# MLP up units: three of four results taken from one running PSUM sum

## The chip, the cores and the metric

The kernel runs on one core of a Trainium2 chip. The metric is the device time of one execution in microseconds (us). TensorE (PE) multiplies matrices into PSUM banks, VectorE (DVE) and ScalarE (ACT) read PSUM and SBUF, GpSimd (POOL) works on SBUF alone, and SyncE (SP) issues the DMAs. Each engine takes its own instructions in a fixed order and waits on semaphores for the others.

## The reference

One layer of a hybrid encoder on x of 2048 tokens by 1024 channels: a mixing half (attention, short convolution, pooling) and then the MLP, which is what the change touches:

```python
h2 = rms_norm(x, norm2_g[l])
f = jnp.square(jax.nn.relu(jnp.einsum('bsd,df->bsf', h2, w_mlp1[l])))
x = x + jnp.einsum('bsf,fd->bsd', f, w_mlp2[l])
```

h2 is 2048 x 1024, w_mlp1 1024 x 4096, w_mlp2 4096 x 1024.

## The kernel before

The first half of the span is the mixing half, which the change leaves alone. The MLP works on tokens in two blocks of 1024 (tb 0 and 1), on the 4096 hidden channels in four chunks (c 0 to 3), and in each chunk first on four **up units** (i 0 to 3, `up`, L995), then on four **down units** (`down`, L1021). So there are 64 units, in the order of the list `units` (L974).

Each unit is a 2 x 2 block product by the seven-product scheme of Strassen and Winograd. Its left operands are sums of weight blocks (a11, a12, a22, s1 to s4) and its right operands sums of data blocks (b11, b21, b22, t1 to t4). Every operand is split into two f16 tiles, high and low, and `product` (L907) multiplies high x high, high x low and low x high for four slices of the inner dimension: twelve matmuls of 128x128 by 128x512 into one PSUM bank. A unit is 84 matmuls. The banks are named b[0] to b[3], each with two buffers, so that the next unit can start while one is read out; b[3] has its own pool (pm1), which opens only after the last step of the mixing half (`stats`, L805) has given its PSUM back.

In `up` the four results are c11 = P(a11) + P(a12); u2 and u3, running sums that start from P(a11) + P(s2); and c21. Before the change ScalarE copies P(a11) out of b[0] (L1001), and VectorE adds every further product from its bank to a tile in SBUF (L1003, L1006, L1008, L1012, L1014: five additions). The product P(a12) is added by TensorE to b[0], which still holds P(a11). Banks b[2] and b[3] are each written twice in a unit. Then ScalarE takes relu (L1017) and square (L1018) of each result, and `data_sums` (L891) makes the seven operands of the down units from them: four subtractions on POOL, and for each operand a cast on ScalarE (L861) and a subtraction on VectorE (L862).

The first time a unit's weights are used (tb 0), `load` (L955) fetches four raw blocks, makes the sums on POOL (`weight_sums`, L868) and splits seven operands (ScalarE L864, VectorE L865), and stores them to `wd` in DRAM. In tb 1 it loads the seven tiles from `wd`, in the order of `WORDER` (L49), into a pool of twelve buffers. The data operands of the MLP's input go through `xd` in DRAM the same way, in the order of `OPS` (L357). At four places (`SPILLS`, L48) `prepare_spill` makes the input operands of tb 1 between units of tb 0. Results and temporaries of the up units share one pool of seven SBUF tiles (`tmp`, L855).

The order of instructions on each engine is not the program's: a scheduler sets it, from its own estimate of when each operand will be there. It moves products ahead of others where it thinks that they would wait.

## Time and profile before

| what | us |
|---|---|
| median of 3 runs | 2141.82 |
| lowest and highest of them | 2135.64, 2143.37 |
| the profiled execution | 2138.21 |
| its span (first to last instruction) | 2136.3 |
| PE busy, share of the span | 96% |
| DVE, ACT, POOL busy | 63%, 48%, 27% |

All that follows is read from the one profiled execution, whose own time lies 3.6 us below the median of the runs. A matmul is recorded with its latency, and matmuls overlap, so a matmul's pace is read from how many fit in a stretch and not from its duration. Idle time that a row gives is the engine's idle time just before the row, with the instruction that ended it.

### The profile page before, as it was taken

To read this page: it belongs to the slowest core of one execution; us is meant where nothing else is said; L and a number is where in the kernel's file an instruction comes from. 1 tells how busy PE (TensorE), PEld (TensorE's weight loads), DVE (VectorE), ACT (ScalarE), POOL (GpSimd) and SP (SyncE) were. 2 spreads that over 40 slices of the span, in tenths; PEclk is the share of its full clock that TensorE was granted. 3 is DMA by queue.
4 is the path that set the end of the run, shared out by engine and by line. 5 is a ranking of instruction groups with operands and counts; after the bars stand their busy time and mean duration, and the time that the engine had idled before them with its cause. 6 is when DMAs were issued, how large, how long until landed. Compare 5 with 4: busy or idle time off the path is not lost. (4 is left out here: it accounts for less than half of the span.)

```text
span 2136.3 us, 31619 instructions
## 1 busy us (share of the span) xinstructions
PE 2041.8 (96%) x11072; PEld 1257.2 (59%) x11072; DVE 1337.3 (63%) x2208; ACT 1016.4 (48%) x2028; POOL 575.8 (27%) x441
## 2 busy tenths in 40 slices
PE   8999898999999898998999999999999999999999
PEld 6777787887787687764444444444444444444444
DVE  6676466756676677767768779767743053353354
ACT  5466575666564454535656456456143151150330
POOL 1110012000210133154556456446422031130132
PEclk9999999999999999999999999999999999999999
DMA  9676797668854687493465555548733333333344
GB/s 318 195 226 210 225 276 238 203 219 265 269 177 124 194 263 209 156 340 115 166 228 186 182 198 187 183 148 295 250 121 104 101 102 104 99 99 107 101 151 150
DMA packets 219567, 399.69 MB, mean 187 GB/s; under 512 B 26000, under 2 KB 33296, under 8 KB 219408
## 3 DMA queue, kind: packets, MB, share of 16 engines
q1 hardware_dynamic: 219408, 397.68, 58.0%
q8 instruction: 87, 1.43, 0.3%
q14 instruction: 72, 0.59, 0.1%
HBM read 275.42 MB, written 105.38 MB: 178 GB/s over the span
## 5 line engine op out<-in xcount | busy, mean ns | idle before, releaser
L911 PE MATMUL b_d<-ft_u,s_d 128*128 128x512 f16 x1152 | 264.1, 379 | 7.3 <-ACT ft_u L861 3.2
L911 PEld LDWEIGHTS <-s_d 128*128 128x128 f16 x1536 | 150.2, 98 | 188.6 <-issue 7.3
L911 PEld LDWEIGHTS <-s_u 128*128 128x128 f16 x1536 | 150.7, 98 | 186.1 <-issue 6.8
L911 PE MATMUL b_u<-zt,s_u 128*128 128x512 f16 x1152 | 257.2, 381 | 1.5 <-DVE u2u L1014 0.8
L1032 DVE TENSOR_TENSOR acc<-acc,b_d 128x512 f32<-128x512 f32 x176 | 119.1, 682 | 178.8 <-PE b_d L911 175.6
L911 PEld LDWEIGHTS <-a_u 128*128 128x128 f16 x1152 | 112.8, 98 | 144.6 <-issue 11.4
L911 PEld LDWEIGHTS <-a_d 128*128 128x128 f16 x1152 | 112.6, 98 | 144.8 <-issue 9.8
L911 PE MATMUL b_d<-fb_u,a_d 128*128 128x512 f16 x768 | 183.7, 379 | 4.2 <-DVE acc L1032 2.0
L911 PE MATMUL b_u<-zb,a_u 128*128 128x512 f16 x768 | 176.7, 379 | 1.3 <-ACT u2u L1001 1.3
L611 ACT ACTIVATE sb<-sb,nm 128x640 f32<-128x640 f32 (+4 forms) x128 | 97.5, 762 | 143.2 <-DVE nm L605 135.2
L895 POOL TENSOR_TENSOR t1u<-u2u,c11u 128x512 f32<-128x512 f32 x32 | 43.7, 1366 | 443.4 <-ACT u2u L1018 443.4
L181 PE MATMUL a<-wq,xg 128*128 128x512 f32 x384 | 153.2, 399 | 0.5 <-DVE wq L161 0.4
L180 PE MATMUL a<-wq,xg 128*128 128x512 f32 x384 | 145.0, 402 | 8.5 <-ACT wq L160 8.5
L182 PE MATMUL a<-wq,xg 128*128 128x512 f32 x384 | 152.8, 399 | 0.0
L243 POOL TENSOR_TENSOR acc<-acc,sq 128x512 f32<-128x512 f32 x28 | 37.6, 1342 | 366.2 <-ACT sq L242 351.6
L605 DVE CUSTOM_DVE_ANT_0 sb<-s,b 128x640 f32<-128x640 f32 (+4 forms) x128 | 94.1, 735 | 66.5 <-PE s L602 65.8
L624 DVE SCALAR_TENSOR_TENSOR pp<-pt,pp 128x384 f16<-128x384 f32 (+1 forms) x224 | 104.0, 484 | 44.5 <-ACT pp L623 44.0
L180 PE MATMUL o<-mix,wo 128*128 128x512 f32 x256 | 107.3, 420 | 0.5 <-DVE gb L760 0.5
L180 PE MATMUL cp<-xg,wc 128*128 128x512 f32 x256 | 107.5, 420 | 0.0
L161 DVE TENSOR_TENSOR wq<-rwq,wq 128x512 fp32r<-128x512 f32 x96 | 68.0, 715 | 62.7 <-ACT wq L160 62.7
L623 ACT ACTIVATE pp<-pt 128x384 f16<-128x384 f32 (+1 forms) x224 | 90.8, 430 | 33.3 <-PE pt L622 32.7
L182 PE MATMUL o<-mix,wo 128*128 128x512 f32 x256 | 102.4, 400 | 0.0
(273 smaller groups left out, 4289.8 us busy)
## 6 DMA issues: line engine op xcount, KB each, us to landing
rwq<-w_qkv SPq DMA_DIRECT2D x96, 256.0 KB, 2.9
p<-w1t SPq DMA_DIRECT2D x64, 256.0 KB, 4.1
rwc<-w_cp SPq DMA_DIRECT2D x64, 256.0 KB, 4.3
rwo<-w_out SPq DMA_DIRECT2D x64, 256.0 KB, 4.2
t<-w SPq DMA_DIRECT2D x64, 256.0 KB, 3.8
r_u<-w SPq DMA_DIRECT2D x64, 256.0 KB, 3.0
wd<-s_u SPq DMA_DIRECT2D x64, 256.0 KB, 2.3
r_d<-w SPq DMA_DIRECT2D x64, 256.0 KB, 2.9
```

The source lines that it names most:

```text
L161: behind(ve.tensor_tensor(out=w[:, 1], in0=raw, in1=w[:, 0].bitcast(F32), op=ALU.subtract))
L180: te.matmul(out, ah, bh, start=start, stop=False)
L181: te.matmul(out, ah, bl, start=False, stop=False)
L182: anchor.append(te.matmul(out, al, bh, start=False, stop=stop).ins.name)
L243: gp.tensor_tensor(out=acc, in0=acc, in1=q, op=ALU.add)
L605: ve.tensor_tensor_reduce(out=sb[:, :nk].rearrange("p (e k) -> p e k", e=ne), in0=s[:, :ne, :hk], in1=bi[:, 640 - nk :].rearrange("p (e k) ...
L611: sc.activation(sb[:, :nk], sb[:, :nk], AF.Exp, bias=nmx, scale=-1.0, accum_out=st["l"][:, i, j : j + 1])
L623: sc.activation(pp[:, 0, c0:c1], pt[:, :n], AF.Copy, scale=PSC)
L624: ve.scalar_tensor_tensor(out=pp[:, 1, c0:c1], in0=pt[:, :n], scalar=PSC, in1=pp[:, 0, c0:c1], op0=ALU.mult, op1=ALU.subtract)
L895: gp.tensor_tensor(out=t1, in0=b12, in1=b11, op=ALU.subtract)
L911: te.matmul(bank, w[:, a, q * P : (q + 1) * P], xs[q][:, c], start=start and q == 0 and i == 0, stop=q == n - 1 and i == 2, skip_group_che ...
L1032: ve.tensor_tensor(out=a, in0=a, in1=bk, op=ALU.add)
```

## The change

In the up unit the products come in another order: a11, s1, s2, a12, s3, s4, a22. P(a11), P(s2), P(s3) and P(a22) are now all added up by TensorE in b[0], one after the other. Between them ScalarE copies the state of the sum out: after P(a11) into c11, after P(s2) into u2, after P(s3) into u3; the last state is c21, which the relu reads from b[0]. The bank b[2] holds P(s1) alone, which VectorE adds to u2 and to u3; b[1] holds P(a12), b[3] holds P(s4). Each of the banks b[1] to b[3] is written once in a unit. VectorE has four additions in place of five, ScalarE three copies in place of one. A product into b[0] has to wait until the copy before it has read the bank. The order in which weights and input operands are stored and loaded follows the new order of products for the up units; the down units keep theirs.

```diff
-WORDER = ("a11", "s2", "s3", "s1", "a12", "a22", "s4")
+WORDER = {"u": ("a11", "s1", "s2", "a12", "s3", "s4", "a22"), "d": ("a11", "s2", "s3", "s1", "a12", "a22", "s4")}
...
-    OPS = ("b11", "t2", "t3", "t1", "b21", "t4", "b22")
+    OPS = ("b11", "t1", "t2", "b21", "t3", "b22", "t4")
...
         product(b[0], w["a11"], xs("b11"), True)
+        c11 = tmp("c11" + nm)
+        sc.copy(c11, b[0])
+        product(b[2], w["s1"], xs("t1"), True)
+        product(b[0], w["s2"], xs("t2"), False)
         u2 = tmp("u2" + nm)
         sc.copy(u2, b[0])
-        product(b[1], w["s2"], xs("t2"), True)
-        ve.tensor_tensor(out=u2, in0=b[1], in1=u2, op=ALU.add)
-        product(b[2], w["s3"], xs("t3"), True)
+        product(b[1], w["a12"], xs("b21"), True)
+        ve.tensor_tensor(out=c11, in0=b[1], in1=c11, op=ALU.add)
+        product(b[0], w["s3"], xs("t3"), False)
         u3 = tmp("u3" + nm)
-        ve.tensor_tensor(out=u3, in0=b[2], in1=u2, op=ALU.add)
-        product(b[3], w["s1"], xs("t1"), True)
-        ve.tensor_tensor(out=u3, in0=b[3], in1=u3, op=ALU.add)
-        product(b[0], w["a12"], xs("b21"), False)
-        product(b[2], w["a22"], xs("t4"), False)
+        sc.copy(u3, b[0])
+        ve.tensor_tensor(out=u2, in0=b[2], in1=u2, op=ALU.add)
+        product(b[3], w["s4"], xs("b22"), True)
+        ve.tensor_tensor(out=u3, in0=b[2], in1=u3, op=ALU.add)
+        ve.tensor_tensor(out=u2, in0=b[3], in1=u2, op=ALU.add)
+        product(b[0], w["a22"], xs("t4"), False)
         c21 = tmp("c21" + nm)
-        ve.tensor_tensor(out=c21, in0=b[2], in1=u2, op=ALU.add)
-        product(b[3], w["s4"], xs("b22"), False)
-        ve.tensor_tensor(out=u2, in0=b[3], in1=u2, op=ALU.add)
-        c11 = tmp("c11" + nm)
-        for src, dst in ((b[0], c11), (u3, u3), (c21, c21), (u2, u2)):
+        for src, dst in ((c11, c11), (u3, u3), (u2, u2), (b[0], c21)):
```

The scheduler moves instructions in answer, and three places show how. A matmul row names bank and unit (`b0_u_0_1_2` is b[0] of up unit 2 of chunk 1 in tb 0), data operand and weight operand; of each run of matmuls of one product the first is shown.

TensorE before, where the up units of chunk 1 in tb 0 end and the down units (`_d_`) begin:

```order
L911 MATMUL b0_u_0_1_3_13139<-zb11_0_0_10952,a11_u0_1_3_12886 128x512
...
L911 MATMUL b0_u_0_1_2_12966<-zb21_0_0_11108,a12_u0_1_2_12717 128x512
...
L911 MATMUL b2_u_0_1_2_12968<-zt4_0_0_11141,a22_u0_1_2_12724 128x512
...
L911 MATMUL b3_u_0_1_2_12969<-zb22_0_0_11175,s4_u0_1_2_12734 128x512
...
L911 MATMUL b3_u_0_1_3_13142<-zt1_0_0_11072,s1_u0_1_3_12893 128x512
...
L911 MATMUL b0_d_0_1_0_13312<-fb11_u_0_1_0_12677,a11_d0_1_0_13108 128x512
...
L911 MATMUL b0_u_0_1_3_13139<-zb21_0_0_11108,a12_u0_1_3_12890 128x512
...
L911 MATMUL b2_u_0_1_3_13141<-zt4_0_0_11141,a22_u0_1_3_12897 128x512
...
L911 MATMUL b3_u_0_1_3_13142<-zb22_0_0_11175,s4_u0_1_3_12907 128x512
...
L911 MATMUL b1_d_0_1_0_13313<-ft2_u_0_1_2_13092,s2_d0_1_0_13126 128x512
```

TensorE at the same place now:

```order
L911 MATMUL b0_u_0_1_3_13146<-zb11_0_0_10952,a11_u0_1_3_12892 128x512
...
L911 MATMUL b0_u_0_1_2_12972<-zt2_0_0_11028,s2_u0_1_2_12736 128x512
...
L911 MATMUL b0_u_0_1_2_12972<-zt3_0_0_11108,s3_u0_1_2_12732 128x512
...
L911 MATMUL b3_d_0_1_0_13323<-ft1_u_0_1_0_12695,s1_d0_1_0_13122 128x512
...
L911 MATMUL b0_u_0_1_2_12972<-zt4_0_0_11175,a22_u0_1_2_12729 128x512
...
L911 MATMUL b0_d_0_1_0_13320<-fb11_u_0_1_0_12682,a11_d0_1_0_13115 128x512
...
L911 MATMUL b0_u_0_1_3_13146<-zt2_0_0_11028,s2_u0_1_3_12910 128x512
...
L911 MATMUL b0_u_0_1_3_13146<-zt3_0_0_11108,s3_u0_1_3_12906 128x512
...
L911 MATMUL b0_u_0_1_3_13146<-zt4_0_0_11175,a22_u0_1_3_12903 128x512
...
L911 MATMUL b0_d_0_1_0_13320<-fb21_u_0_1_0_12688,a12_d0_1_0_13119 128x512
```

The steps of unit 2's running sum now stand late and close together: nothing stands between its s2 and its s3 product, and two matmuls of a down unit between s3 and a22.

ScalarE at this place before, from the casts of the spill (`yt`) to the first relu of unit 2's c11:

```order
L861 CAST yt2_1_1_12958<-x2_1_5_1_12930 128x512
L1018 ACTIVATE u3u_0_1_2_13009<-u3u_0_1_2_13009 128x512
L861 CAST yt4_1_1_12962<-x2_1_5_0_12927 128x512
L864 ACTIVATE a11_d0_1_0_13108<-r0_d0_1_0_13098,sw_120 128x512
L864 ACTIVATE a12_d0_1_0_13112<-r1_d0_1_0_13100,sw_120 128x512
L864 ACTIVATE s1_d0_1_0_13115<-s1_d0_1_0_13106,sw_120 128x512
L864 ACTIVATE a22_d0_1_0_13119<-r3_d0_1_0_13104,sw_120 128x512
L864 ACTIVATE s3_d0_1_0_13122<-r2_d0_1_0_13102,sw_120 128x512
L1017 ACTIVATE c11u_0_1_2_13063<-b0_u_0_1_2_12966 128x512
```

ScalarE there now:

```order
L1005 COPY u2u_0_1_2_13014<-b0_u_0_1_2_12972 128x512
L861 CAST fb11_u_0_1_2_13079<-c11u_0_1_2_12988 128x512
L861 CAST yt2_1_1_12964<-x2_1_5_1_12936 128x512
L861 CAST yt4_1_1_12968<-x2_1_5_0_12933 128x512
L864 ACTIVATE a11_d0_1_0_13115<-r0_d0_1_0_13105,sw_120 128x512
L864 ACTIVATE a12_d0_1_0_13119<-r1_d0_1_0_13107,sw_120 128x512
L864 ACTIVATE s1_d0_1_0_13122<-s1_d0_1_0_13113,sw_120 128x512
L1010 COPY u3u_0_1_2_13041<-b0_u_0_1_2_12972 128x512
```

Six instructions now stand between the copies of u2 and of u3 of this unit.

TensorE at the end of the mixing half before, with the products around the two matmul groups of `stats` (ms2_3 and rb23):

```order
L911 MATMUL b2_u_0_0_2_11634<-zt3_0_0_11028,s3_u0_0_2_11442 128x512
...
L248 MATMUL ms2_3_11202<-ones_96,acc23_8559 128x1 x4
...
L911 MATMUL b2_u_0_0_2_11634<-zt3_0_3_11034,s3_u0_0_2_11442 128x512
L256 MATMUL rb23_11223<-ident_87,r1r_11211 128x128 x4
...
L911 MATMUL b3_u_0_0_0_11289<-zt1_0_0_11072,s1_u0_0_0_10898 128x512
```

TensorE there now:

```order
L911 MATMUL b2_u_0_0_2_11636<-zt1_0_0_10989,s1_u0_0_2_11436 128x512
...
L248 MATMUL ms2_3_11202<-ones_96,acc23_8559 128x1 x4
...
L911 MATMUL b2_u_0_0_2_11636<-zt1_0_3_10995,s1_u0_0_2_11436 128x512
...
L911 MATMUL b1_u_0_0_2_11635<-zb21_0_0_11072,a12_u0_0_2_11433 128x512
...
L256 MATMUL rb23_11223<-ident_87,r1r_11211 128x128 x4
...
L911 MATMUL b3_u_0_0_0_11289<-zb22_0_0_11141,s4_u0_0_0_10912 128x512
```

Between ms2_3 and rb23 there stood one matmul, and now stand thirteen, the twelve of the a12 product of unit 2 among them.

## Rows read from the trace of the kernel before

**Rows 1.** The profile's page: span, and busy time of each engine with its share.

```profile
span 2136.3 us, 31619 instructions
PE 2041.8 (96%) x11072; PEld 1257.2 (59%) x11072; DVE 1337.3 (63%) x2208; ACT 1016.4 (48%) x2028; POOL 575.8 (27%) x441
```

**Rows 2.** Busy time in stretches, one per chunk: tb 0's four, then two of tb 1.

```profile
core 0: us, PE busy (x) PEld busy (x) DVE busy (x) ACT busy (x) POOL busy (x), PEclk, DMA share, GB/s
971.00:1094.40 123.40, 118.52 (x541) 52.94 (x540) 97.74 (x108) 75.59 (x129) 68.39 (x45) 0.99 0.50 171
1094.40:1250.00 155.60, 148.22 (x673) 66.14 (x672) 126.25 (x153) 81.76 (x135) 84.80 (x57) 0.99 0.57 194
1250.00:1403.20 153.20, 146.31 (x673) 65.73 (x672) 120.35 (x144) 77.47 (x127) 78.24 (x54) 1.00 0.52 176
1403.20:1552.00 148.80, 145.64 (x673) 65.71 (x672) 109.19 (x137) 65.71 (x109) 76.60 (x52) 1.00 0.68 241
1552.00:1697.10 145.10, 145.10 (x674) 65.78 (x673) 44.87 (x58) 49.10 (x83) 22.93 (x16) 1.00 0.35 106
```

**Rows 3.** Waits of TensorE from 971 to 1552: total us, times, longest.

```profile
PE b_u L911 <- DVE u3u L1006: 5.0, 3, 2.0
PE b_d L911 <- DVE acc L1032: 3.8, 3, 2.0
PE b_d L911 <- ACT ft_u L861: 3.2, 5, 1.0
PE b_d L911 <- DVE ft_u L862: 1.9, 2, 1.0
PE b_u L911 <- DVE u3u L1008: 1.8, 3, 1.2
PE b_d L911 <- DVE fb_u L862: 1.6, 2, 1.2
PE b_u L911 <- ACT u2u L1001: 1.3, 1, 1.3
PE b_d L911 <- DVE c21u L1012: 1.2, 1, 1.2
PE b_u L911 <- DVE u2u L1014: 0.8, 1, 0.8
...
PE b_d L911 <- ACT fb_u L861: 0.7, 1, 0.7
```

**Rows 4.** TensorE in order of time, tb 0 chunk 1: start, length, count, idle before.

```profile
1151.20 4.44 PE L911 MATMUL b_u<-zt,a_u 128*128 128x512 f16 x12 [2.04 <-DVE u3u L1006]
1155.48 2.75 PE L911 MATMUL b_u<-zb,s_u 128*128 128x512 f16 x12
```

**Rows 5.** All engines in order of time, end of the mixing half.

```profile
968.70 1.16 PE L256 MATMUL rb<-ident,r1r 128*128 128x128 f32 x8 [2.85 <-DVE r1r L207]
969.95 0.59 ACT L814 COPY r2s<-rb 128x512 f32<-128x512 f32 x1 [3.34 <-PE rb L256]
970.59 6.91 PE L911 MATMUL b_u<-zt,s_u 128*128 128x512 f16 x24 [0.73 <-ACT r2s L814]
```

**Rows 6.** Instructions on tile u2u: count, duration in ns (least, median, most).

```profile
L1001 ACT COPY u2u<-b_u x32: 560/586/587, 917.3 to 2044.3; 128x512 f32<-128x512 f32 x32
L1014 DVE TENSOR_TENSOR u2u<-b_u,u2u x32: 673/691/692, 980.1 to 2059.9; 128x512 f32<-128x512 f32 x32
L1018 ACT ACTIVATE u2u<-u2u x32: 612/629/632, 981.5 to 2061.4; 128x512 f32<-128x512 f32 x32
L895 POOL TENSOR_TENSOR t1u<-u2u,c11u x32: 1258/1269/1803, 984.4 to 2062.1; 128x512 f32<-128x512 f32 x32
L861 ACT CAST ft_u<-u2u x32: 617/618/626, 989.1 to 2064.8; 128x512 f16<-128x512 f32 x32
```

**Rows 7.** Groups of ScalarE in chunk 1 of tb 0: count, busy us, mean ns.

```profile
L864 ACT ACTIVATE a_d<-r_d,sw 128x512 f16<-128x512 f32 x12 | 8.4, 715 | 3.8 <-PE b_d L911 3.7
```

**Rows 8.** All engines in order of time, first down unit of chunk 1.

```profile
1180.06 0.68 DVE L1014 TENSOR_TENSOR u2u<-b_u,u2u 128x512 f32<-128x512 f32 x1
1187.27 1.26 POOL L895 TENSOR_TENSOR t1u<-u2u,c11u 128x512 f32<-128x512 f32 x1
```

**Rows 9.** The DMA view: issues of weight tiles, KB each, us to landing.

```profile
a_u<-wd SPq DMA_DIRECT2D x48, 256.0 KB, 2.6
```

More of the change, by code (lines that the diff above doesn't have):

```diff
@@ L951, in trunk @@
     NU = FF // 256 // NC
-    wd = dram.tile([2, NC, 4, len(WORDER), P, 1024], F16, name="wd")
+    wd = dram.tile([2, NC, 4, 7, P, 1024], F16, name="wd")
     def load(u):
@@ L960, in load @@
             o = {}
-            for n, op in enumerate(WORDER):
+            for n, op in enumerate(WORDER[kind]):
                 o[op] = wp.tile([P, 2, 512], F16, tag="w", name=f"{op}_{nm}")
@@ L969, in load @@
             o = weight_sums([w2[c, i, 0], w2[c, i, 1], w2[c, i + 4, 0], w2[c, i + 4, 1]], sw[:, 1:2], nm)
-        for n, op in enumerate(WORDER):
+        for n, op in enumerate(WORDER[kind]):
             sy.dma_start(kept[n], o[op].rearrange("p a b -> p (a b)"))
```

## Prediction

> **What bounds the kernel now.** I read the busy shares first: TensorE is busy 96% of the span, VectorE 63%, ScalarE 48% [rows 1]. That says only that TensorE's idle time is the most there is to win. The stretches by chunk then say where it lies [rows 2]. A chunk is 8 units, 672 matmuls. In tb 1 a chunk takes 145.1 us with TensorE busy throughout: 0.216 us a matmul, 2.59 us a product. There nothing can be gained, whatever VectorE is spared, and a new wait shows in full. In tb 0 the same work takes 155.6, 153.2 and 148.8 us in chunks 1 to 3: 10.5, 8.1 and 3.7 us more. Chunk 0's 541 matmuls would take 116.7 us and took 123.4: 6.7 us more. So 29 us are lost in tb 0, and 2.85 us just ahead of it, where TensorE waits for the statistics of the mixing half [rows 5]. These 32 us, 1.5% of the span, are the whole stake.
>
> The waits of TensorE in tb 0 say for whom [rows 3]. Inside the up units the products wait for a bank that VectorE has not read yet, or once for ScalarE's copy: 5.0 + 1.8 + 1.3 + 0.8 = 8.9 us. Where the down units begin they wait for the operands of the last up unit, or for its bank: 3.2 + 1.9 + 1.6 + 1.2 + 0.7 = 8.6 us. The down units' own additions (acc, 3.8 us) are not touched. After one of the long waits twelve matmuls took 4.44 us, the next twelve 2.75 [rows 4], another 1.7 us.
>
> **The change part by part. Work of VectorE and ScalarE.** 32 up units lose one addition each: 32 x 0.69 = 22 us of VectorE; they gain two copies: 64 x 0.586 = 37.5 us of ScalarE [rows 6]. Neither is on the path by its sum. In chunk 1, the fullest, ScalarE goes from 82 to 87 of 155 us, VectorE from 126 to 124 [rows 2]. Relu from PSUM moves from c11 to c21, at no cost. I count these sums at nothing; TensorE's 145 us a chunk hide them.
>
> **Banks written once.** The 8.9 us come from b[2], b[3] and b[0] being written again in the same unit. Now b[1] to b[3] are written once, and the next writer is two units on. In the order the nearest case for b[2] has 15 matmuls, 3.2 us, between the s3 product and the next unit that writes that buffer, against a copy of 0.59 and an addition of 0.69; for b[3] it is 12 matmuls, 2.6 us, against a copy and two additions, 2.0. I take the 8.9 us as gone, and the 1.7 us of slow matmuls with them.
>
> **The step to the down units.** Before, the last product of an up unit, s4, fed u2, and u2 fed t1 and then t2, which the down unit wants in its second product. In chunk 1 the addition to u2 ran at 1180.06 and t1 began at 1187.27 [rows 8]: behind it came two activations, and POOL was late. Now s4's product stands before the chain's end, and a22, the last, feeds b21 and t4 alone. After a22 the order has 30 matmuls, 6.5 us, that need nothing of this unit. The longest path to the first that does is relu, square and cast on ScalarE with six other instructions among them, and a subtraction on VectorE: about 9 x 0.62 + 0.69 = 6.3 us [rows 6]. That is tight, so of the 8.6 us I leave 2 in place and take 6.6.
>
> **The statistics.** Between their two matmul groups the order had one matmul, and now has thirteen, 2.8 us. VectorE's small steps there ended 2.85 us after TensorE fell idle [rows 5]. Twelve more matmuls hide 2.6 of it. The 24 matmuls after the second wait took 6.91 us where two products of twelve [rows 4] follow each other in 2.59 + 2.75 = 5.34; I take these 1.6 us as gone too. The 0.73 us of the copy remain.
>
> Removed: 8.9 + 1.7 + 6.6 + 2.6 + 1.6 = 21.4 us.
>
> **The running sum's waits.** Each unit now has three points where a product into b[0] waits for a copy: 96 in all. The trace has one such handover with nothing to hide it: the matmuls of rb end at 969.86, ScalarE copies from 969.95 for 0.59, the next matmul starts at 970.59, 0.73 us idle [rows 5]. What stands between the two products in the order decides. After a11 it is at least 21 matmuls (4.5 us) everywhere. Of the 96, 82 have 12 or more between (2.59 us), so 1.86 us are left over, three instructions of ScalarE's queue. Fourteen have less: two have none, two have 2, four (tb 1, the last unit of each chunk, s3 to a22) have 3, six have 6. With ScalarE free they cost 2 x 0.73, 2 x 0.30, 4 x 0.08 and 0, together 2.4 us: the lower end.
>
> ScalarE's queue is not free in tb 0. In chunk 1's unit 2 six instructions stand between the copies of u2 and u3: three casts and three weight splits, 3 x 0.62 + 3 x 0.715 = 4.0 us [rows 6, 7]. The s3 product and two matmuls take 3.0; with the copy's 0.59 that is a wait of 1.6 us. It repeats in chunk 2. For the six with 6 matmuls I take 0.3 each, for the four of tb 1 0.25 each (an odd instruction ahead of the copy every other time). Sum: 2 x (0.73 + 1.6) + 1.8 + 1.0 = 7.5 us. Two products of the first down unit are drawn ahead in chunks 1 and 2, and their weights are split by then only just; 1 us each. Together 9.5 us. The upper end, every one of the 14 behind four instructions of 0.62, is 14 x 2.5 = 35 us.
>
> The wait itself holds all that follows on TensorE; on ScalarE the casts and splits behind a copy wait for TensorE, on VectorE the splits behind the first addition to u2 wait for the copy. The next in line is the bank b[0] itself: at six places the down unit writes it 6 matmuls (1.3 us) after a22, against a relu of 0.59 to 0.63; I count nothing for it.
>
> The Trainium skill speaks against this layout: PSUM — Partial Sum Buffer, Summary: rules for kernel authors, says that PSUM read while matmuls run should be in a bank other than the one they write. That rule would make every handover a stop: 96 x 0.73 = 70 us, 2138.2 - 21.4 + 70 = 2187. The order puts products into other banks between nearly all of them, so this has 0.01 of the third rival's chance below. ScalarE: Activation LUTs, Rules for kernel authors, gives about 0.3 us and 0.83 ns an element for an ACTIVATE, an estimate of 0.72 us for these 512 columns; the rows show 0.586 for the copies. By the page's price the eight shortest handovers would cost 1.1 us more.
>
> **DMAs.** No load or store is added; they follow the new order. The tightest weight load has 24 matmuls, 5.2 us, from its buffer's release to its first use, and lands in 2.6 us [rows 9]. Nothing.
>
> **Sum.** 21.4 - 9.5 = 11.9 us off the span: 2136.3 becomes 2124.4, the execution's 2138.21 becomes 2126.3. The median of the runs lies 3.6 us above that execution, so it may come out a little higher; I write 2126.
>
> **The rivals.** First: the new waits take back what the old ones gave. ScalarE's queue already holds casts that wait for POOL and DMA, so a copy behind them comes late; and where VectorE is late in a spill, its lateness moves to the down units' first operands. For it: 14 close handovers, most in the chunks that lose most today. Against it: ScalarE idles 47% of chunk 1. With new waits of 18 us in place of 9.5 the gain is 3.4, 2134.8. A measurement of this kernel tells about 0.5%, 10.7 us, from no change, so this reads as the same.
>
> Second: TensorE's order is kept by tb 1 as well, where nothing is idle now, and the down unit's matmuls drawn into the up units break its even run: 1.5 us at each of four chunks, with the first rival's tb 0: 2141. Also the same.
>
> Third, slower: the copies of u2 and u3 in tb 0's 16 units, 32 handovers, each stand behind weight splits and casts so that TensorE waits 1.3 us beyond its cover, 42 us, and the old waits go all the same: 2138.2 - 21.4 + 42 = 2159. It decides from 1.0 us each (32 us), where the loss passes 10.7. Against it: in the order only 10 of the 32 have under 12 matmuls of cover.
>
> That the change does not do what it says is no case: the order shows 32 fewer instructions on VectorE and 64 more on ScalarE.
>
> **How the numbers follow.** My own case, new waits under 10.7 and so a gain from 10.7 to 19 us: 0.53. The first rival 0.28, the second 0.10, the third 0.09. Faster by over 0.5%: 0.53; within: 0.38; slower: 0.09. The range goes from all that is removed with the lower end of the new waits, 2138.2 - 21.4 + 2.4 = 2119, less 4 us because the runs shown spread over 7.7 us: 2115; up to the second rival's 2141. What is left out, the third rival and a tenth of the rest, is under 2 in 10.
>
> **What would show it.** In the changed kernel's stretches by chunk, chunks 1 and 2 of tb 0 should take about 150 us, chunk 0 about 120, tb 1's 145 to 146.5. The waits of TensorE should have no u3u or c21u addition of VectorE inside up units, and new ones on ScalarE's copies, some 8 us in all, the longest at the end of chunks 1 and 2. The wait for r1r should be under 0.5 us. Waits on the copies over 20 us, or tb 1 chunks over 147 us, would make the forecast wrong.

## The result: 1.3% slower, all of it in three chunks

The changed kernel takes 2163.2 us (median of 4 runs, 2161.5 to 2172.1), beside 2138.7 for the kernel before: a ratio of 1.0128, 95% interval 1.0083 to 1.0173 (the two medians alone give 1.0115; the kernel before has four executions here, the three of its table and one more). The forecast was 2126 with a range from 2115 to 2141. The profiled span is 2161.3 us, 25.0 above the 2136.3 of [rows 1].

The page of the changed kernel, its span and its engines:

```profile
span 2161.3 us, 31624 instructions
PE 2055.0 (95%) x11072; PEld 1262.1 (58%) x11072; DVE 1336.0 (62%) x2176; ACT 1046.5 (48%) x2092; POOL 574.8 (27%) x441
```

VectorE has the 32 instructions fewer and ScalarE the 64 more that the change promised. VectorE's busy time fell by 1.3 us, not by the 22 of 32 additions: other instructions of it became longer (VectorE beside GpSimd, below).

The stretches by chunk, with the columns of [rows 2]: tb 0's chunks 0 to 3, and the first of tb 1.

```profile
970.40:1093.60 123.20, 116.88 (x529) 51.91 (x529) 90.66 (x102) 76.47 (x132) 66.19 (x44) 0.99 0.51 168
1093.60:1260.80 167.20, 151.38 (x673) 66.85 (x672) 132.73 (x151) 86.63 (x144) 84.41 (x57) 0.97 0.54 182
1260.80:1421.80 161.00, 150.94 (x674) 66.95 (x673) 126.17 (x141) 82.01 (x135) 78.99 (x54) 0.97 0.50 168
1421.80:1576.30 154.50, 147.78 (x673) 65.87 (x672) 113.38 (x133) 69.52 (x117) 76.84 (x52) 0.99 0.68 232
1576.30:1721.50 145.20, 145.17 (x673) 65.77 (x672) 42.09 (x54) 52.37 (x91) 22.87 (x16) 1.00 0.36 106
```

Beside [rows 2], chunk 1 went from 155.6 to 167.2, chunk 2 from 153.2 to 161.0, chunk 3 from 148.8 to 154.5: 25.1 us, the whole difference. Tb 1 went from 145.1 to 145.2, chunk 0 stayed at 123. Of the 25.1 us, 9.9 are busy time of TensorE (450.1 in place of 440.2 in the three chunks) and 15.2 are idle. The mean granted clock fell to 0.97 in chunks 1 and 2, so part of them ran at the lower of the two levels (1.2 and 2.4 GHz). The slow matmuls stand behind the long waits:

TensorE in order of time, chunk 1 and chunk 2: start, length, count, idle before. The last line is a stretch behind the first wait, with the columns of [rows 2]: the granted clock in it is 0.50.

```profile
1158.57 4.44 PE L911 MATMUL b_u<-zt,s_u 128*128 128x512 f16 x12 [5.28 <-ACT u2u L1005]
1165.71 1.01 PE L911 MATMUL b_d<-ft_u,s_d 128*128 128x512 f16 x2 [2.71 <-DVE u2u L1014]
...
1325.46 4.44 PE L911 MATMUL b_u<-zt,s_u 128*128 128x512 f16 x12 [4.93 <-ACT u2u L1005]
```

```profile
1158.70:1162.10 3.40, 3.40 (x9) 1.21 (x8) 3.40 (x4) 2.08 (x4) 2.69 (x3) 0.50 0.40 148
```

The waits of TensorE from 970 to 1576 (two under 1 us left out), beside [rows 3]:

```profile
PE b_d L911 <- DVE acc L1033: 11.0, 7, 3.6
PE b_u L911 <- ACT u2u L1005: 10.2, 2, 5.3
PE b_d L911 <- DVE ft_u L862: 7.5, 10, 1.3
PE b_d L911 <- DVE u2u L1014: 5.4, 2, 2.7
PE b_d L911 <- DVE s_d L865: 2.8, 1, 2.8
PE b_u L911 <- DVE u2u L1014: 1.2, 1, 1.2
```

The waits for u3 and c21 are gone. In their place stand two waits for ScalarE's copy of u2 (one in chunk 1, one in chunk 2), and TensorE waits longer for most of what VectorE gives the down units: acc 11.0 us in place of 3.8, the splits ft_u 7.5 in place of 1.9.

What ScalarE, VectorE and GpSimd wait for in the three chunks (1093.6 to 1576.3), some of the lines: total us, times, longest. The last two lines are the kernel before, the same stretch.

```profile
ACT c21u L1018 <- PE b_u L911: 28.2, 11, 3.8
```

```profile
DVE s_u L865 <- ACT s_u L864: 25.7, 14, 4.2
...
DVE x L925 <- DMA rr<-r2d: 13.3, 2, 6.8
```

```profile
POOL u3u L899 <- DVE fb_u L862: 27.3, 11, 7.5
```

```profile
DVE s_u L865 <- ACT s_u L864: 14.3, 16, 1.9
```

```profile
ACT ft_u L861 <- POOL t1u L895: 28.5, 12, 4.1
```

The reader is to see the first line: ScalarE stood 28 us at c21's relu, which now reads the bank of the unit's last product itself. What stands behind that relu in ScalarE's queue waits with it. The last line is a caution: the kernel before has a wait as long on ScalarE, at the cast for t1, which is made from the unit's last product there. A long wait at the head of a queue is not a loss by itself; what stands behind it decides.

The long wait of chunk 1, seen on ScalarE and VectorE in order of time:

```profile
1142.75 0.60 ACT L1018 ACTIVATE c21u<-b_u 128x512 f32<-128x512 f32 x1 [3.70 <-PE b_u L911]
...
1156.38 0.63 ACT L1018 ACTIVATE c11u<-c11u 128x512 f32<-128x512 f32 x1 [2.80 <-DVE c11u L1007]
...
1157.95 0.56 ACT L1005 COPY u2u<-b_u 128x512 f32<-128x512 f32 x1
```

```profile
1145.16 1.42 DVE L925 SCALAR_TENSOR_TENSOR x<-x,g2s,rr 128x512 f32<-128x512 f32 x2 [6.77 <-DMA rr<-r2d]
...
1155.67 0.68 DVE L1007 TENSOR_TENSOR c11u<-b_u,c11u 128x512 f32<-128x512 f32 x1
```

VectorE waits 6.8 us with a spill's multiplication at its head, works off the splits of the unit before and the spill, and reaches the addition to c11 at 1155.67. ScalarE has c11's relu at its head and stands 2.8 us; u2's copy is behind it.

### The profile page after: what moved, and what is told of

Same layout as the page of the kernel before. It is cut to its first block, busy times and chain, and to the rows that moved or that the text cites. A ratio compares the mean times of both kernels' runs of the same rounds, so it can differ in the third digit from the quotient of the medians.

```text
span 2161.3 us, 31624 instructions
## 1 busy us (share of the span) xinstructions
PE 2055.0 (95%) x11072; PEld 1262.1 (58%) x11072; DVE 1336.0 (62%) x2176; ACT 1046.5 (48%) x2092; POOL 574.8 (27%) x441
## 5 line engine op out<-in xcount | busy, mean ns | idle before, releaser
L911 PE MATMUL b_u<-zt,s_u 128*128 128x512 f16 x1152 | 274.2, 387 | 10.2 <-ACT u2u L1005 10.2
L911 PEld LDWEIGHTS <-s_u 128*128 128x128 f16 x1536 | 152.2, 99 | 199.9 <-issue 24.8
L1033 DVE TENSOR_TENSOR acc<-acc,b_d 128x512 f32<-128x512 f32 x176 | 117.9, 681 | 145.0 <-PE b_d L911 143.2
L911 PE MATMUL b_u<-zb,a_u 128*128 128x512 f16 x768 | 182.6, 379 | 0.0
L181 PE MATMUL a<-wq,xg 128*128 128x512 f32 x384 | 152.8, 398 | 0.4 <-DVE wq L161 0.4
L182 PE MATMUL a<-wq,xg 128*128 128x512 f32 x384 | 152.2, 398 | 0.0
L180 PE MATMUL o<-mix,wo 128*128 128x512 f32 x256 | 107.3, 420 | 0.5 <-DVE gb L760 0.5
L1007 DVE TENSOR_TENSOR c11u<-b_u,c11u 128x512 f32<-128x512 f32 x32 | 22.0, 687 | 137.1 <-PE b_u L911 68.6
```

The source lines that it names most:

```text
L180: te.matmul(out, ah, bh, start=start, stop=False)
L181: te.matmul(out, ah, bl, start=False, stop=False)
L182: anchor.append(te.matmul(out, al, bh, start=False, stop=stop).ins.name)
L911: te.matmul(bank, w[:, a, q * P : (q + 1) * P], xs[q][:, c], start=start and q == 0 and i == 0, stop=q == n - 1 and i == 2, skip_group_che ...
L1033: ve.tensor_tensor(out=a, in0=a, in1=bk, op=ALU.add)
```

## The experiments

Seven explanations were put to the test. Their letters stand in the expectations: **V**, VectorE is late because a spill's work stands ahead of the unit's additions; **A**, u2's copy stands behind c11's relu on ScalarE; **O**, the products in their new order make the instruction order draw the next unit's products ahead, so that units end later; **H**, the handovers of b[0] themselves; **W**, weight tiles are freed in another order than they are taken; **P**, VectorE's splits are slower beside GpSimd; **S**, ScalarE's queue stands at c21's relu with finished work behind it.

Each ratio goes by the executions of the kernel before that stood beside, whose median was 2138 to 2143 us. A chunk is counted from the first matmul of its first up unit to that of the next chunk's, in the order of time of TensorE, in the one profiled execution of each kernel. How well such a column repeats shows where an edit touches nothing: e1 leaves chunk 3 alone, and it took 155.3 us there beside 154.5.

| kernel | median us | ratio to before (95%) | c 1 | c 2 | c 3 | tb 1 |
|---|---|---|---|---|---|---|
| before | 2138.7 | | 155.6 | 153.2 | 148.8 | 145.0 |
| changed | 2163.2 | 1.0128 (1.0083 to 1.0173) | 167.2 | 161.0 | 154.5 | 145.2 |
| e1, spill behind unit | 2171.2 | 1.0141 (1.0089 to 1.0192) | 168.4 | 165.7 | 155.3 | 145.2 |
| e2, spills in down halves | 2160.0 | 1.0084 (1.0061 to 1.0107) | 154.5 | 159.1 | 163.0 | 145.2 |
| b2, before, the same | 2140.8 | 1.0004 (0.9985 to 1.0023) | 149.3 | 156.8 | 153.7 | 145.0 |
| e3, u2's copy first | 2164.1 | 1.0108 (1.0075 to 1.0141) | 164.6 | 159.6 | 154.7 | 145.2 |
| e4, order alone | 2155.0 | 1.0063 (1.0041 to 1.0084) | 160.8 | 157.6 | 153.6 | 145.0 |
| e12, bank alone | 2168.0 | 1.0119 (1.0095 to 1.0144) | 168.1 | 160.8 | 155.5 | 145.2 |
| e5, units in turn | 2159.3 | 1.0103 (1.0077 to 1.0129) | 160.6 | 155.9 | 155.2 | 145.2 |
| e5b, unit 3 too | 2155.5 | 1.0082 (1.0061 to 1.0103) | 161.2 | 158.5 | 155.1 | 145.2 |
| e6, order alone, in turn | 2168.8 | 1.0142 (1.0115 to 1.0168) | 163.8 | 163.4 | 158.1 | 145.0 |
| e7, splits in product order | 2170.2 | 1.0156 (1.0124 to 1.0189) | 168.5 | 160.2 | 154.5 | 145.2 |
| e8, e5b and e3 | 2155.2 | 1.0060 (1.0038 to 1.0082) | 161.0 | 157.6 | 152.2 | 145.2 |
| e9, e5b and e2 | 2157.0 | 1.0068 (1.0049 to 1.0088) | 155.4 | 154.4 | 161.3 | 145.2 |
| p1, half of GpSimd's sums | 2153.0 | 1.0051 (1.0029 to 1.0074) | 158.1 | 157.4 | 152.8 | 145.4 |
| p0, before, the same | 2122.8 | 0.9910 (0.9882 to 0.9938) | 149.4 | 148.9 | 146.6 | 145.0 |
| e10, c21 last | 2149.8 | 1.0034 (1.0013 to 1.0055) | 156.0 | 155.1 | 156.0 | 145.0 |
| e11, e10 and e5b | 2150.4 | 1.0048 (1.0030 to 1.0066) | 158.5 | 158.6 | 154.3 | 145.0 |
| v1, before, sums on VectorE | 2130.1 | 0.9946 (0.9928 to 0.9965) | 154.5 | 149.1 | 146.3 | 145.0 |
| v2, e10, sums on VectorE | 2143.3 | 1.0003 (0.9989 to 1.0016) | 159.1 | 152.8 | 149.3 | 145.0 |

### The spill: where it stands, and whether it is there

e1 writes the spill behind the up unit:

```diff
-        if n in SPILLS:
+        if n in SPILLS and kind == "d":
             prepare_spill(1, SPILLS.index(n))
...
             F.append(up(u, w, X))
+            if n in SPILLS:
+                prepare_spill(1, SPILLS.index(n))
```

> The changed kernel, with the preparation of token block 1's operands (the spill) written behind the up unit instead of ahead of it, in chunks 1 and 2. Theory V (VectorE's queue): the spill's four multiplications by rr stand ahead of the unit's c11 addition in VectorE's queue and wait 6.8 us for a transfer; ScalarE's copies queue behind that. Then the waits of 5.3, 2.7, 1.4 and 1.1 us and the slow matmuls behind them go in chunks 1 and 2: chunk 1 from 167 to 155 to 157, chunk 2 from 161 to 149 to 152, the whole 2138 to 2146. Theory A (ScalarE's queue: u2's copy stands behind c11's relu) expects the same here, since the addition is no longer late. Theory O (the new product order leaves TensorE nothing to draw on): both chunks stay within 2 us, 2158 to 2164.

e2 and b2 move the spills out of the up halves, in the changed kernel and in the one before:

```diff
-SPILLS = (6, 10, 14, 18)
+SPILLS = (6, 14, 21, 23)
```

> The changed kernel, with the two spills of the up halves of chunks 1 and 2 moved to the down half of chunk 2 (SPILLS 6, 14, 21, 23 in place of 6, 10, 14, 18). Theory V: no up unit has a spill's multiplications ahead of its additions; chunk 1 falls from 167 to about 156, the up half of chunk 2 has no wait over 1 us, its down half takes two spills at about 5 us of waits each (as chunk 1's down half shows now): chunk 2 near 159; the whole 2146 to 2152. Theory O: the up halves still wait 8 us or more; 2158 to 2164.

> The kernel before, with SPILLS 6, 14, 21, 23 as in the changed kernel's run. If a spill in an up half costs this kernel as it costs the changed one (chunk 1 fell by 12.8 us there, chunks 2 and 3 gave back 6.6), it falls by 2 to 8 us, 2133 to 2140; if the queues of the kernel before took its spills in the up halves without loss, the crowded down half of chunk 2 makes it slower, 2143 to 2152.

V in its simple form fell. With unit 2's additions ahead of the spill on VectorE chunk 1 took 168.4 us, VectorE's wait for rr was gone, and TensorE waited at about the same time for the copies of the next unit:

```profile
1160.69 4.98 PE L911 MATMUL b_u<-zt,s_u 128*128 128x512 f16 x12 [5.07 <-ACT c11u L1001]
1169.66 5.28 PE L911 MATMUL b_u<-zt,s_u 128*128 128x512 f16 x12 [3.99 <-ACT u2u L1005]
```

With no spill in its up half (e2) chunk 1 falls by 12.8 us. But so does the kernel before fall in its chunk 1, by 6.4 (b2). Chunks 2 and 3, where the spills went, together give back about half of it in e2 and more than all of it in b2. The excess over the kernel with the same spills is 5.2, 2.3 and 9.3 us in chunks 1 to 3: it moved with the spills, and two thirds of it remained. A spill makes the loss larger; most of the loss does not need one in an up half.

### The two parts of the change apart

e4 has the new order of products with the sums of before (c11 kept in b[0], u2 copied, five additions). e12 has the running bank and its copies with the products written and stored in the old order:

```diff
         product(b[0], w["a11"], xs("b11"), True)
+        sc.copy(c11, b[0])
+        product(b[0], w["s2"], xs("t2"), False)
+        sc.copy(u2, b[0])
+        product(b[0], w["s3"], xs("t3"), False)
+        sc.copy(u3, b[0])
+        product(b[2], w["s1"], xs("t1"), True)
...
+        product(b[1], w["a12"], xs("b21"), True)
...
+        product(b[0], w["a22"], xs("t4"), False)
+        product(b[3], w["s4"], xs("b22"), True)
```

> The order of the seven products and of the stored operands as in the changed kernel, but the sums as in the kernel before: one copy (u2), five additions on VectorE, c11 = p1 + p2 kept in the bank, no running bank. Theory O: the order is the cause; chunks 1 and 2 stay near 167 and 161, the whole 2155 to 2164. Theories V and A, which put the loss to the copies behind the c11 addition that VectorE makes: 2134 to 2144, as the kernel before, with chunk 1 at 154 to 158. A time over 2150 with chunk 1 over 162 would speak against both.

> The kernel before with the running bank and its copies alone: products written and stored in the old order (a11, s2, s3, s1, a12, a22, s4), of which a11, s2, s3 and a22 add up in one bank, c11 and u3 copied too, four additions on VectorE. If the bank's chain of dependent products by itself makes the order on TensorE and ScalarE's waits (theories O and S together), it loses as the changed kernel does, whatever the written order: 2156 to 2168, chunk 1 at 162 to 169, chunk 3 at 153 to 156. If the written order is what costs (by the run of the order alone, 14 of 24 us), the bank alone costs the remaining 8 to 10: 2146 to 2152.

The parts do not add. The order alone costs 0.63%, the bank alone 1.19%, both 1.28%. e12 answers a question that the diff hides: its products are written in the old order, yet as the program comes out TensorE draws those of chunk 1's units in the same order as in the changed kernel, almost to the matmul. Three of the sum's steps wait for a copy, and the instruction order fills the gaps with the next unit's products, in both written orders. Its waits are the changed kernel's too:

```profile
ACT c21u L1018 <- PE b_u L911: 27.5, 11, 4.0
```

```profile
PE b_u L911 <- ACT u2u L1004: 10.7, 2, 5.5
```

e4 loses at the same place by another wait, one for VectorE, since its s3 and a22 products now follow each other into b[2]:

```profile
1161.41 4.75 PE L911 MATMUL b_u<-zt,a_u 128*128 128x512 f16 x12 [5.16 <-DVE u3u L1008]
```

### Units in turn

In chunk 1 of the kernel before, unit 1's last product is the 14th that TensorE does; in the changed kernel it is the 19th. e5 ties units 1 and 2 behind the unit ahead, e5b (shown) unit 3 as well; e6 ties units 1 and 2 of the order alone:

```diff
                 mm = te.matmul(bank, ...)
+                if held and q == 0 and i == 0:
+                    follow(tc, mm.ins, held[0])
+        last[:] = [mm.ins.name]
...
+            if tb == 0 and c > 0 and i in (1, 2, 3):
+                held[:] = last
             F.append(up(u, w, X))
+            held.clear()
```

> The changed kernel, with order-only dependencies on TensorE: in chunks 1 to 3 of token block 0 every product of up units 1 and 2 stands behind the last product of the unit ahead, as it already did in the kernel before. Theory O (the new product order makes the instruction order draw the next unit's products ahead, so that unit 1 ends four products later and VectorE's work of all that follows is late): the pile-up in front of the spill goes; chunk 1 from 167 to 153 to 158, chunk 2 from 161 to 150 to 155, chunk 3 from 154.5 to about 150, the whole 2137 to 2148; the back-to-back handovers of the running bank then show as waits of ScalarE's copies of 0.7 to 2 us each. Theory H (the handovers of the running bank are what costs): these handovers now have nothing between them and cost 4 to 6 us a chunk more, 2170 or above. Theory W (the stored weights are freed in another order than their tiles are taken): no change beyond 3 us a chunk, 2155 to 2163.

> As the run with units 1 and 2 in turn, with unit 3 behind unit 2 as well. Theory O: VectorE's work is as even as there, but the end of the up half has nothing to draw on but the down products, so 1 to 4 us a chunk above that run: 2140 to 2158. Theory H: six more handovers with nothing between, 2172 or above. Theory W: as that run, 2155 to 2163.

> The product order alone (the sums of the kernel before, 2155 on the chip), with the same order-only dependencies on TensorE as in the run with units 1 and 2 in turn. Theory O: its 14 us over the kernel before go, 2137 to 2146, chunk 1 at 154 to 158. Theory W: the order in which the weights are freed is unchanged, so 2150 to 2158. Theory H has nothing to say of this kernel, which has no running bank.

O holds a part at most: chunk 1 falls by 6 us, chunk 2 by 2.5 to 5, chunk 3 not at all, and the whole by 4 to 8 us by the medians, with intervals that overlap the changed kernel's. H fell as the cause: with handovers next to each other the whole got no slower. They are not free, though. With ScalarE free one costs what a copy takes, as u3's here in e5b; but the waits for u2's and u3's copies in e5b's three chunks come to 25.3 us (17.3 of them in the second line), and other waits fell by more:

```profile
1110.25 2.75 PE L913 MATMUL b_u<-zt,a_u 128*128 128x512 f16 x12 [0.67 <-ACT u3u L1015]
```

```profile
PE b_u L913 <- ACT u2u L1010: 17.3, 8, 5.1
```

For e6 O expected a cure and got 0.8% more loss: units in turn put that kernel's s3, a22 and s4 products next to each other, and it waits for VectorE (18.4 us in ten waits over the three chunks, the longest 3.4).

### Smaller suspects

e3 puts c11's relu behind u2's copy, e8 does so with units in turn, e7 writes the splits of an up unit's weights in the order of its products, e9 joins units in turn and spills in the down halves:

```diff
-        sc.copy(u2, b[0])
+        got = sc.copy(u2, b[0])
...
-            sc.activation(dst, src, AF.Relu, scale=2.0**-19)
+            ins = sc.activation(dst, src, AF.Relu, scale=2.0**-19)
+            if dst is c11:
+                follow(tc, ins.ins, got.ins.name)
```

> The changed kernel, with one order-only dependency more: c11's relu stands behind u2's copy in ScalarE's queue. Theory A: ScalarE copies u2 as soon as its product ends, so the two waits of 5.28 and 4.93 us fall below 1 us and the slow matmuls behind them go; the whole 2147 to 2153. Theory V: VectorE is as late as before; the wait for the copy goes, but the wait for the bank that VectorE frees with u2 += b3 (2.71 us now) grows by most of it; 2155 to 2163.

> The changed kernel with the up units 1 to 3 in turn on TensorE (2155.5 by itself) and c11's relu behind u2's copy on ScalarE. With the units in turn two waits of about 5 us for u2's copy are left, one in chunk 1 and one in chunk 2, each beside a spill. Theory A (the copy stands behind c11's relu, which waits for VectorE's late addition): these two fall under 1.5 us and the slow matmuls behind them go; 2144 to 2150. Theory V (VectorE's queue is late by the spill whatever ScalarE does): the wait moves to the next thing that VectorE gives, 2152 to 2157.

> The changed kernel, with the splits of an up unit's weights written in the new order of its products (a11, s1, s2, a12, s3, s4, a22), so that tiles are taken in the order in which they are freed. Theory W: chunks 1 to 3 fall by 4 us or more each, the whole 2140 to 2150. Theory O: the units are drawn into each other as before, 2156 to 2166.

> The changed kernel with the up units 1 to 3 in turn and no spill in an up half (SPILLS 6, 14, 21, 23). Theory O and V together (units late by the drawing ahead, VectorE late by the spill): up halves with nothing but the back-to-back handovers, 1 us or so each, six a chunk; chunk 1 at 151 to 154, chunk 2 at 152 to 157, chunk 3 at 152 to 156 (a spill runs into its start), the whole 2140 to 2150. If VectorE's load in the down halves is the limit by itself, the down halves take back what the up halves give: 2153 to 2160, as the changed kernel with its spills in the down halves.

A fell as the whole cause. In e3 the waits for the copy shrink to 0.9 and 0.7 us, and 9 us after the first TensorE waits longer than ever, again for ScalarE:

```profile
1162.59 1.03 PE L911 MATMUL b_d<-ft_u,s_d 128*128 128x512 f16 x2 [6.13 <-ACT s_d L864]
```

In e8, too, waits of 4.5 and 4.3 us for the copy stayed, with c11's relu out of its way. Ahead of the copy that came at 1150.33 stood this cast, and another that waited 2.2 us, both for sums of GpSimd:

```profile
1145.93 0.62 ACT L861 CAST ft_u<-u3u 128x512 f16<-128x512 f32 x1 [4.73 <-POOL u3u L899]
```

W fell (e7, no better). e9 gave nearly what V and O promised together in chunks 1 and 2 (155.4 and 154.4), and chunk 3 took it back with the spill that runs into it.

In e5b's chunk 3, which has no spill, the rows show what is left. ScalarE, VectorE and GpSimd at the end of the up half:

```profile
1495.10 0.63 ACT L1024 ACTIVATE u3u<-u3u 128x512 f32<-128x512 f32 x1
1500.07 0.60 ACT L1023 ACTIVATE c21u<-b_u 128x512 f32<-128x512 f32 x1 [4.34 <-PE b_u L913]
1500.57 0.71 ACT L864 ACTIVATE s_d<-s_d,sw 128x512 f16<-128x512 f32 x1
...
1502.35 0.61 ACT L861 CAST fb_u<-u3u 128x512 f16<-128x512 f32 x1
```

```profile
1501.31 0.75 DVE L865 SCALAR_TENSOR_TENSOR s_d<-s_d,sw,s_d 128x512 f16<-128x512 f32 x1 [5.11 <-ACT s_d L864]
```

```profile
1505.07 1.27 POOL L878 TENSOR_TENSOR s_d<-r_d,r_d 128x512 f32<-128x512 f32 x1 [7.75 <-DVE ft_u L862]
1506.30 1.26 POOL L899 TENSOR_TENSOR u3u<-u3u,t1u 128x512 f32<-128x512 f32 x1
```

u3 is finished at 1495.7. Its cast and a weight's cast stand behind c21's relu, which waits for TensorE until 1500.07; VectorE then waits 5.1 us for the weight's cast; GpSimd stands 7.8 us at a weight's sum until VectorE's splits run again, and u3's sum is behind it. From this chunk theory S was made.

### c21 handled last

Only two of the down units' seven operands need c21. e10 writes the square, casts and sums of the other results ahead of c21's relu; e11 adds units in turn:

```diff
+        for t in (c11, u3, u2):
+            square(t, t)
+        o = {"b11": mk(c11, "b11")}
...
+        o["b22"] = mk(u3, "b22")
+        gp.tensor_tensor(out=u3, in0=u3, in1=t1, op=ALU.subtract)
+        o["t1"] = mk(t1, "t1")
+        o["t3"] = mk(u2, "t3")
+        o["t2"] = mk(u3, "t2")
+        square(b[0], c21)
+        o["b21"] = mk(c21, "b21")
+        gp.tensor_tensor(out=c21, in0=c21, in1=u3, op=ALU.subtract)
+        o["t4"] = mk(c21, "t4")
```

> The changed kernel, with c21 (the result of the last product, a22) handled last in each up unit: the casts and sums of c11, u3 and u2 are written ahead of c21's relu, square and splits, which only two of the seven operands need. Theory S (ScalarE's queue stands at c21's relu, with work of the finished results and of the next weights behind it): the 28 us of waits of c21's relu in chunks 1 to 3 stay but have little behind them; GpSimd's wait for the u3 split (27 us in 11) falls under 10, the last splits of chunk 3's up half come at 90 to 93 us of the chunk in place of 97.7, chunk 3 falls from 154.5 to 149 to 151, the whole to 2145 to 2154. Theories O and V (drawing ahead, the spill): chunks 1 to 3 within 2 us of 167, 161 and 154.5, the whole 2157 to 2165.

> Both edits: up units 1 to 3 in turn on TensorE (2155.5 by itself) and c21 handled last. Theory S: in this order c21's relu waits 4 us a unit with the u3 split and a weight cast behind it (chunk 3: GpSimd waits 7.8 us for it), so the gain is as large as without units in turn: 2138 to 2148, chunk 3 at 149 to 151, the last splits of its up half at 90 to 93 in place of 98.3. Theory V: VectorE is late by the spills and by the weights whatever the order of the splits; 2152 to 2157.

e10 is the largest single cure among the kernels that leave nothing out: 1.0034 in place of 1.0128, 13 us by the medians, intervals apart, with the running bank and the written order of its products untouched, and with the up units' products in nearly the same order on TensorE (the interval of e8 overlaps e10's). Chunk 1 falls by 11.2 us, chunk 2 by 5.9, together 17 of their 19.4. The waits of e10's chunks 1 to 3 moved in part as S said. ScalarE's wait of c21's relu for TensorE, which S expected to stay, is in no line any more, and of VectorE and GpSimd we read

```profile
DVE s_u L865 <- ACT s_u L864: 10.4, 8, 1.8
```

```profile
POOL u3u L1029 <- DVE fb_u L862: 2.1, 3, 0.7
POOL c21u L1035 <- DVE fb_u L862: 39.0, 11, 4.8
```

The first two stand in place of 25.7 and 27.3. But the third is new: GpSimd's wait did not go, it moved to c21's sum, the last of the unit, and VectorE's wait for the casts of ft_u grew from 1.8 to 18.6 us (21.0 in the kernel before). So a good part of the waits moved to places with less behind them. Of the expectation's numbers two more were missed: chunk 3 stays at 156.0 in place of 149 to 151, and its up half's last split comes at 97.4 us of the chunk, as before the edit (97.7; in the kernel before it came at 88.0). In a chunk 3, where S had been read off, its cure gave nothing. Units in turn add nothing to e10 (e11).

Two more limits. The wait at the relu does not measure the loss: units in turn cut it from 28.2 us to the 10.8 of the line below in e5, and e5 still loses 1.03% (14 of the 25 us by the chunk columns). And the same edit was not made to the kernel before, so what part of the 13 us it would give there too is not shown.

```profile
ACT c21u L1023 <- PE b_u L913: 10.8, 10, 1.9
```

### VectorE beside GpSimd

VectorE's splits of the up results have both inputs in SBUF. The addition that ends u2 and the split of u2 in the changed kernel: count, duration in ns (least, median, most). The last line is the split in v1 (below), where GpSimd does not make these sums.

```profile
L1014 DVE TENSOR_TENSOR u2u<-b_u,u2u x32: 675/681/693, 974.0 to 2088.2; 128x512 f32<-128x512 f32 x32
```

```profile
L862 DVE TENSOR_TENSOR ft_u<-u2u,ft_u x32: 679/1623/1765, 981.5 to 2099.0; 128x512 f16<-128x512 f32 x32
```

```profile
L862 DVE TENSOR_TENSOR ft_u<-u2u,ft_u x32: 674/682/686, 991.6 to 2059.5; 128x512 f16<-128x512 f32 x32
```

The addition that reads PSUM never takes longer than 0.69 us; the split takes 0.68 or up to 1.77. The Trainium skill says why in SBUF — State Buffer, Who interferes with whom: a VectorE instruction with two SBUF inputs contends with a GpSimd instruction that reads SBUF, over a port pair that the two share. The traces agree by these rows: with GpSimd's sums gone the same split takes 0.68 us every time. In chunks 1 to 3 VectorE was busy 372.3 us in place of 355.8, with 10 instructions fewer. p1 and p0 make three of the four sums of each up unit over half the columns and leave the other half out, so that they do not compute the layer and serve for the time alone, in the changed kernel and in the one before; v1 and v2 give all four to VectorE (of the kernel before, and of e10):

```diff
-        gp.tensor_tensor(out=b12, in0=b22, in1=b12, op=ALU.subtract)
+        gp.tensor_tensor(out=b12[:, :h], in0=b22[:, :h], in1=b12[:, :h], op=ALU.subtract)
```

> The changed kernel, with three of GpSimd's four sums of each up unit's results made over 256 of 512 columns (the other half is left as it is, so these sums are incomplete). Theory P: VectorE's operations whose operands all lie in SBUF take 1.75 us instead of 0.68 beside a running GpSimd, and the changed kernel puts 20 us more of that into chunks 1 to 3; half of GpSimd's time then gives VectorE back 8 to 12 us of busy time in these chunks, and the whole falls by 10 us or more, to 2145 to 2153, and by more than the kernel before gains by the same edit. Theories O, V, A: only the latency of the sums is saved (3 x 0.8 us a unit), hidden but at the hand-over to the down half, 2154 to 2162.

> The kernel before with the same edit: three of GpSimd's four sums of each up unit's results over 256 of 512 columns. Theory P: it has less of VectorE's splits beside GpSimd, so it gains less than the changed kernel does: 2 to 5 us, 2133 to 2138. Theories O, V, A: as much as the changed kernel gains, or 2 to 6 us by the hand-over to the down halves.

> The kernel before, with the four sums of each up unit's results made by VectorE instead of GpSimd. Theory P (the slow-down beside GpSimd and the hops between engines cost more than the sums): 12 units x 4 sums x 0.68 us = 33 us more work on VectorE in chunks 1 to 3, and some 25 to 30 us less of slow splits; the chain from an up unit to its splits shortens by 4 x 1 us; 2118 to 2132, faster than the kernel before. If VectorE's amount of work is what counts: 2145 to 2165.

> The changed kernel with c21 handled last, and the four sums of each up unit's results made by VectorE. It has 12 additions fewer on VectorE in chunks 1 to 3 (8 us). Theory P: as the kernel before with the same edit or a little better, 2115 to 2132, with chunk 3 falling from 156 to 147 to 151. If VectorE's amount of work is what counts: 2150 to 2170.

As the cause of the loss P fell: the changed kernel gains 0.8% by half the sums, the kernel before 0.9%, so the distance stays. In p1 VectorE is busy 350.7 us in the three chunks, less than the kernel before, and they still take 468 us in place of 458. Nor does VectorE's amount of work bound these chunks. In v1 it grew by 22 us, to 377, while they took 449.8:

```profile
1097.00:1546.80 449.80, 439.22 (x2017) 197.33 (x2016) 377.35 (x483) 223.62 (x372) 169.34 (x114) 1.00 0.61 207
```

v1 is a version that beats both kernels: 2130.1 us, 0.9946 of the kernel before, interval 0.9928 to 0.9965. v2 brings the changed kernel level with the one before, and its chunk 3 from 156.0 to 149.3; beside v1, which is its like, it is still 13 us slower by the medians.

## Why the prediction was wrong, point by point

**"Relu from PSUM moves from c11 to c21, at no cost."** This is the step that failed, and with it the reckoning that the other engines' work is hidden (next point). I priced the move by the duration of the instruction, which did not change, and not by what waits behind it. c11's relu read a bank whose product stood ahead of two others, and no wait of it for TensorE is in tb 0 of the kernel before; c21's reads that of the last product, and ScalarE stood 28 us in 11 waits for it. e10 writes the finished work ahead of c21's relu, square, casts and sum; that gave back 13 of the 24.5 us. How much of the 13 is the relu's wait and how much GpSimd's and VectorE's new order, which e10 changes with it, was not taken apart, and the other 11 us are open.

**"I count these sums at nothing; TensorE's 145 us a chunk hide them."** As sums, rightly: p1 and v1 show that a chunk is not bound by VectorE's amount of work. (Its size was off too: VectorE in chunk 1 was to go from 126 to 124 us and went to 132.7, by the slower splits.) But casts, splits and sums pass between three engines with fixed queues, and the question was what stands at each head, not how full a queue is.

**The old bank waits, 8.9 us, gone.** Right for the waits named (u3, c21, u2's copy before a12). VectorE's last addition to u2 then cost TensorE 5.4 + 1.2 us, where 2.0 us of work had 2.6 of cover: the estimate took VectorE as on time.

**The slow matmuls, 1.7 us, gone.** Wrong in sign: after the 5 us waits twelve matmuls took 4.44 us again, now in chunk 1 and in chunk 2, and TensorE's busy time in the three chunks grew by 9.9.

**The step to the down units, 6.6 us of 8.6 gone.** Wrong. The path after a22 was counted from a free ScalarE; the waits there are now 7.5 + 2.8 us, on VectorE's splits of results and weights, and with the 5.4 for the bank 15.7, where 2 were left in place and 2 counted for the products drawn ahead.

**The statistics, 2.6 us.** Right in place and size:

```profile
968.47 1.16 PE L256 MATMUL rb<-ident,r1r 128*128 128x128 f32 x8 [0.26 <-DVE r1r L207]
```

2.85 us in [rows 5]. The matmuls behind it were not slow any more either (36 in 7.93 us). Chunk 0 as a whole gained next to nothing.

**The new waits on copies, 7.5 us.** Measured 10.2, in unit 2 of chunks 1 and 2, as said. The term was near by luck: it put 0.73 us on the handover from s2 to s3 and 1.6 on that from s3 to a22; the trace has 5.3 and 4.9 on the first and none on the second. What held the copies in the changed kernel were not casts but c11's relu waiting for VectorE. A copy took 0.56 to 0.59 us, as the rows had it. The rule of the Trainium skill (PSUM — Partial Sum Buffer, Summary: rules for kernel authors), to read PSUM in another bank than the running matmuls write, was rightly set aside as a price by the rows: tb 1 has 48 handovers and takes 145.2 us a chunk in place of 145.0.

**"The down units' own additions are not touched."** They went from 3.8 to 11.0 us. VectorE reaches them late; that the splits ahead of them in its queue, late themselves, hold them up is my reading of the order and was not tested.

**The sum.** The forecast took 7.7 us off beyond the statistics (8.9 + 1.7 + 6.6 less 9.5); chunks 1 to 3 of tb 0 alone became 25.1 us longer. Four of the terms above make about these 33 us: the step to the down units 11.7 (15.7 in place of 4), the slow matmuls 11.6 (9.9 more in place of 1.7 less), the down units' additions 7.2, the copies 2.7.

The first rival came nearest in kind: in the changed kernel a copy came late behind waiting work on ScalarE, and VectorE's lateness reached the down units' first operands. It gave this 18 us of new waits, too little for a loss. The second rival (tb 1's rhythm) did not come. The third had the sign and nearly the time, 2159, by a mechanism that did not occur: the copies' waits were 10 us, not 42. What I had named as signs of failure, copies over 20 us or tb 1 over 147, stayed quiet; a sign on chunks 1 to 3 alone would have spoken.

**What stays open.** Chunk 3's 5.7 us: neither c21 last nor units in turn moved them. They lie in the down half, where TensorE waits for acc:

```profile
1548.56 4.03 PE L911 MATMUL b_d<-fb_u,a_d 128*128 128x512 f16 x12 [3.42 <-DVE acc L1033]
```

With the sums on VectorE in both kernels the distance of chunk 3 falls to 3.0 (149.3 and 146.3), which points to the path through GpSimd; but chunks 1 and 2 then keep 4.6 and 3.7, so the three together are 11.3 us apart, no less than e10 is from the kernel before (9.5). What makes this rest was not found. GpSimd's waits for the raw weight blocks in chunks 1 to 3 are 62.0 us in the changed kernel, 39.5 in the one before and 28.9 in e10; whether they are cause or consequence is open too. The spill's wait for rr is less of a suspect: in e1, e2, e7 and p1 it is in no line of VectorE's waits, and they lose all the same. Chunk 0, which shares its start with the mixing half, took 188 to 198 us in these profiles for reasons I did not follow; a difference of 5 us between two totals is therefore read from the chunk columns.

## What to carry to other kernels

When an instruction on a queue engine is moved to read a later product, its own duration tells nothing: list what is finished and stands behind it, and who waits for that. A chain of dependent sums in one bank can set TensorE's order by itself: two written orders came out nearly the same here. Where a stretch is loose on every engine's sum, look at the head of each queue and at what is behind it; handling the last result last was worth more to the changed kernel here than any other single edit that leaves nothing out.

## What the chip showed that I had not expected

Two parts of a change that cost 0.63% and 1.19% alone cost 1.28% together: either way TensorE stands some 5 us near the end of chunk 1's up units, for VectorE in the one and for ScalarE in the other. VectorE did more work and the kernel was faster: 48 sums in three chunks moved from GpSimd added 22 us to VectorE's busy time there, where 48 x 0.68 = 33 would be expected, and took 7.8 us off the chunks. And a wait of 5 us costs TensorE some 1.7 us more behind it (4.44 us for twelve matmuls in place of 2.75), at a granted clock of 0.50 there and 0.97 for the chunk.
